# Hybrid encoder block on one core: low halves of the front-half weights subtracted on VectorE instead of GpSimd

## Chip, cores and metric

One core of a Trainium2 chip. The metric is the device time of one execution in microseconds. Engines are called PE (TensorE), DVE (VectorE), ACT (ScalarE), POOL (GpSimd) and SP (the queue that issues the DMAs).

## What is computed

One layer of a streaming encoder on 1024 tokens of width 1024, all in f32:

```
h = x @ w_in
ya = chunked attention over 8 heads, with a relative bias
yb = gated, 31-tap causal depthwise convolution, LayerNorm, swish
yc = gated DeltaNet, 4 heads, chunks, sequential state
mix = sum_b sigmoid(gate_b) * (y_b @ w_branch[b])
x = LN1(alpha * x + mix @ w_out)
x = LN2(alpha * x + relu(x @ w_up)^2 @ w_down + sigmoid(x @ w_pg) * (p @ w_pp))
```

## The kernel before, in words

**Split products.** A matmul takes its operands as fp32r. To keep f32 accuracy each operand is held as a high part, `hi`, the copy rounded to fp32r, and a low part, `lo = src - hi`; a product is three matmuls: hi by hi, hi by lo, lo by hi. The helper `split_lo(eng, lo, src, hi)` (L115, subtraction on L116) makes the low part on whichever engine is passed: `V` is VectorE, `G` is GpSimd.

**Weights of the front half.** `wload` (L118) takes a raw, a hi and a lo tile from a pool (2 raw, 6 hi and 6 lo buffers; 2 of each for the side products by `fload`, L137) and calls `wsplit` (L126): DMAs into raw on SP (L131), the hi copy on ACT (L133), the low part on GpSimd (L134). Each tile holds 512 columns by 128 partitions, 528 in `v_proj(0)`. The products `v_proj` (tiles wv), `qk_proj` (wq, wk), `dn_proj` (wc), the side products `side_glu` and `side_proj` (fa, fg) and `merge` (wbr) all come this way. Outside it are the first product, `z_start`, and everything after the merge: the output projection, the gate product and the MLP, which use other helpers, some with GpSimd.

**Order of the work.** The program is written as stages: z; attention (four pairs of heads); DeltaNet, head by head; merge of the three branches; output projection and what follows. The framework's scheduler makes each engine's list from this, with a priority by the place in the program and a model of what each operation takes. Each engine then executes its list strictly in order. The side products are given the lowest priority, so they are filled in wherever the list of PE would otherwise wait: their 1600 matmuls and transposes (PSUM tiles fj, tb, tq) lie among attention and DeltaNet and are used up before the merge is under way.

**A DeltaNet head.** `dn_proj` makes c (q, k, v after a 4-tap convolution on DVE, L431, L435). `dn_s1` transposes them (PSUM tiles tk, L480, and tv, L490) and makes the chunk matrices. `dn_inv` inverts 32x32 blocks by 31 steps on DVE, each L553 and then L554 on the tiles tm and X. `dn_s2` puts the inverse together (px, py, L578). `dn_scan` walks 8 chunks: a matmul with the state (L631), a subtraction on DVE (L632), a matmul (L635), the new state on DVE (L640), and the output (L633, L642, then ACT L643, L644). `dn_out` normalises: L648 on DVE, a power on POOL (L190), L655 on DVE, 8 transposes (PSUM tile to, L659), L660 on DVE, and stores to DRAM (yc_d, L661). Meanwhile the inverse of the next head and the product of the one after it run.

**Merge.** `merge(b)` loads a branch's output back from DRAM (`yload`: L719; hi copy on ACT, L720; low part on DVE) as four tiles of 128 rows, and multiplies them by 8 weight tiles, wbr20 to wbr27 for b = 2 (PSUM tile pbr, L164). The fourth tile of branch 2 is the output of the last DeltaNet head, so no product of merge 2 can end before it is there. Four PSUM banks hold these sums.

**The 31-tap convolution** of branch b, `b_conv`, is 240 operations on DVE (L676), also of the lowest priority; softmax rows are scaled on POOL (L307).

Of the kernel before, what the change touches and what calls it, by code (L numbers as in the profile page):

```python
# [54 lines left out]
def hybrid_block(ctx, tc, x, xT, pT, w_in, relb, conv_w, conv_b, cln_g, cln_b, dnw, a_log, dt_bias,  # L55
# [3 lines left out]
    V, S, G, PE, SY = nc.vector, nc.scalar, nc.gpsimd, nc.tensor, nc.sync  # L59
# [26 lines left out]
    def slot(shape, dt=F32, name="g"):  # L86
        return gp.tile(shape, dt, tag="g", bufs=NSLOT, name=name)
# [27 lines left out]
    def split_lo(eng, lo, src, hi):  # L115
        eng.tensor_tensor(lo, src, hi.bitcast(F32), ALU.subtract)  # L116

    def wload(src, kt, cols, name, tag="w", width=528, bufs=(2, 6)):  # L118

        n = kt * cols  # L120
        raw = wp.tile([P, width], F32, tag=tag + "r", bufs=bufs[0], name=name + "r")[:, :n]
        hi = wp.tile([P, width], F32R, tag=tag + "h", bufs=bufs[1], name=name + "h")[:, :n]
        lo = wp.tile([P, width], F32R, tag=tag + "l", bufs=bufs[1], name=name + "l")[:, :n]
        return wsplit(src, raw, hi, lo, kt)

    def wsplit(src, raw, hi, lo, kt):  # L126
        rv = raw.rearrange("p (k c) -> p k c", k=kt)
        c0 = 0
        for s in (src if isinstance(src, list) else [src]):
            w = s.shape[-1]  # L130
            SY.dma_start(rv[:, :, c0:c0 + w], s)  # L131
            c0 += w
        S.activation(hi, raw, AF.Copy)  # L133
        split_lo(G, lo, raw, hi)  # L134
        return hi.rearrange("p (k c) -> p k c", k=kt), lo.rearrange("p (k c) -> p k c", k=kt)

    def fload(src, kt, cols, name):  # L137
# [790 lines left out]
    for k in range(2):  # L928
        hi = slot([P, T], F32R, name="pth")
        lo = slot([P, T], F32R, name="ptl")  # L930
        raw = slot([P, T], name="ptr")
# [436 lines left out]
```

## Time and profile before

| | |
|---|---|
| median of 3 runs | 1928.42 us (1927.6 to 1931.17) |
| profiled execution, its own time | 1930.17 us |
| span of its trace | 1928.2 us |
| PE busy | 1848.2 us (96%) |
| DVE busy | 1254.8 us (65%) |
| ACT busy | 831.8 us (43%) |
| POOL busy | 449.9 us (23%) |

Stretches and waits are given in us from the start of the span. A busy time is that of an engine's instructions; a wait is idle time of an engine, put down to whatever released it. An engine's `x` counts are instructions; f32 matmuls of 128 columns stand twice in the trace where the program's list has them once.

### The profile page before, as it was taken

The numbers are of one execution on the slowest core, as the hardware profiler recorded it, in microseconds if no ns is written. First come the engines' busy times: TensorE is split into PE (matmuls) and PEld (weight loads), VectorE is DVE, ScalarE is ACT, GpSimd is POOL, SyncE is SP. The second block draws the span as 40 slices with busy tenths as digits, with TensorE's granted clock in tenths as the row PEclk, the third lists the DMA queues.
The fourth block names the chain that finished last, engine by engine and source line by source line (L and its number), as shares of the span: only waits on it lengthen the run. The fifth ranks groups of instructions, "written<-read, shape, count | busy, mean of one in ns | idle before, by whom it ended". The sixth has DMA issues, their size and how long they took to land. (4 is left out here: it accounts for less than half of the span.)

```text
span 1928.2 us, 25795 instructions
## 1 busy us (share of the span) xinstructions
PE 1848.2 (96%) x9265; PEld 1545.3 (80%) x9265; DVE 1254.8 (65%) x2203; ACT 831.8 (43%) x1516; POOL 449.9 (23%) x373
## 2 busy tenths in 40 slices
PE   8999999999998989989999999999999998999996
PEld 7988888778777868777888998678888887878885
DVE  3249859999957856665367548783433336876978
ACT  4454444445324333443354226445555554333333
POOL 2123433234322222222112133222232320000001
PEclk9999999999999989999999999999999999999998
DMA  6212222232342323243364535763232359347133
GB/s 202 82 49 73 74 64 68 71 89 77 87 129 61 98 72 104 66 132 92 125 199 158 168 112 180 267 224 123 96 125 94 126 196 330 139 153 256 72 114 126
DMA packets 207792, 244.67 MB, mean 127 GB/s; under 512 B 23792, under 2 KB 126256, under 8 KB 207664
## 3 DMA queue, kind: packets, MB, share of 16 engines
q1 hardware_dynamic: 207664, 243.03, 39.4%
q8 instruction: 73, 1.20, 0.3%
q14 instruction: 55, 0.45, 0.1%
HBM read 183.17 MB, written 59.80 MB: 126 GB/s over the span
## 5 line engine op out<-in xcount | busy, mean ns | idle before, releaser
L676 DVE SCALAR_TENSOR_TENSOR ca<-ci,cw_s,ca 128x512 f32<-128x512 f32 x240 | 213.3, 889 | 3.8
L986 PE MATMUL pda<-bh,ah 128*128 128x512 f32 x256 | 97.3, 396 | 8.3 <-DVE x L1258 8.3
L987 PE MATMUL pda<-bl,ah 128*128 128x512 f32 x256 | 101.2, 395 | 1.2 <-DVE bl L116 1.2
L190 POOL TENSOR_TENSOR mv<-mv,nhalf 128x1 f32<-128x1 f32 x16 | 19.7, 1235 | 351.7 <-DVE mv L683 351.7
L988 PE MATMUL pda<-bh,al 128*128 128x512 f32 x256 | 101.1, 395 | 0.0
L307 POOL TENSOR_SCALAR st<-st,mx 128x640 f32<-128x640 f32 (+2 forms) x64 | 58.8, 919 | 176.7 <-DVE mx L306 156.6
L304 ACT ACTIVATE st<-st,mx 128x640 f32<-128x640 f32 (+2 forms) x64 | 44.5, 696 | 114.2 <-DVE mx L300 114.1
L1163 DVE TENSOR_TENSOR r<-puc,r 128x512 f32<-128x512 f32 x16 | 11.1, 691 | 106.9 <-PE puc L988 106.9
L986 PE MATMUL pdb<-bh,ah 128*128 128x512 f32 x192 | 72.9, 396 | 6.3 <-ACT bh L1216 5.5
L987 PE MATMUL pdb<-bl,ah 128*128 128x512 f32 x192 | 75.5, 393 | 0.0
L988 PE MATMUL pdb<-bh,al 128*128 128x512 f32 x192 | 75.2, 392 | 0.0
L1216 ACT ACTIVATE ah<-draw 128x1024 fp32r<-128x1024 f32 x30 | 31.8, 1059 | 94.0 <-PE pdb L987 30.9
L986 PEld LDWEIGHTS pda<-bh,ah 128*128 128x128 f32 x256 | 49.1, 192 | 19.2 <-ACT x L1266 4.8
L987 PEld LDWEIGHTS pda<-bl,ah 128*128 128x128 f32 x256 | 49.1, 192 | 11.9 <-DVE bl L116 1.7
L988 PEld LDWEIGHTS pda<-bh,al 128*128 128x128 f32 x256 | 49.0, 191 | 10.4
L554 DVE TENSOR_TENSOR X<-X,tm 32x31 f32<-32x31 f32 (+15 forms) x124 | 51.9, 418 | 3.0
L771 ACT ACTIVATE sgl<-sgl 128x512 f32<-128x512 f32 x48 | 30.2, 631 | 53.4 <-DMA sgl<-sg_d 47.7
L553 DVE TENSOR_TENSOR tm<-X 32x31 f32<-32x31 f32 (+15 forms) x124 | 51.1, 412 | 3.0
L431 DVE SCALAR_TENSOR_TENSOR c<-pc,dnw_s,c 128x511 f32<-128x511 f32 (+2 forms) x72 | 52.5, 731 | 0.1
L116 DVE TENSOR_TENSOR al<-draw,ah 128x1024 fp32r<-128x1024 f32 x30 | 36.5, 1216 | 23.2 <-ACT ah L1216 23.0
L334 ACT ACTIVATE ph<-tp 128x512 fp32r<-128x512 f32 (+2 forms) x72 | 37.0, 525 | 33.4 <-PE tp L330 29.3
L986 PEld LDWEIGHTS pdb<-bh,ah 128*128 128x128 f32 x192 | 36.4, 190 | 14.6 <-ACT bh L1216 6.0
(1609 smaller groups left out, 6190.4 us busy)
## 6 DMA issues: line engine op xcount, KB each, us to landing
draw<-h_d SPq DMA_DIRECT2D x46, 512.0 KB, 5.3
wu<-in_w_up_dram SPq DMA_DIRECT2D x32, 512.0 KB, 3.9
h_d<-r SPq DMA_DIRECT2D x64, 256.0 KB, 2.1
draw<-in_w_down_dram SPq DMA_DIRECT2D x30, 512.0 KB, 4.7
sg_d<-fs SPq DMA_DIRECT2D x48, 256.0 KB, 2.1
sgl<-sg_d SPq DMA_DIRECT2D x48, 256.0 KB, 3.0
wg<-in_w_pg_dram SPq DMA_DIRECT2D x36, 256.0 KB, 4.4
cb<-in_w_down_dram SPq DMA_DIRECT2D x16, 512.0 KB, 8.0
```

The lines of the kernel that those rows point to most:

```text
L116: eng.tensor_tensor(lo, src, hi.bitcast(F32), ALU.subtract)
L304: S.activation(st[:, :nk], st[:, :nk], AF.Exp, scale=-1.0, bias=mx[:, nm:nm + 1], accum_out=mx[:, 2:3])
L307: G.tensor_scalar(st[:, :nk], st[:, :nk], mx[:, 3:4], 1.0, ALU.mult, ALU.mult)
L334: S.activation(ph[:, :n], tp[:, :n], AF.Copy)
L431: V.scalar_tensor_tensor(acc[:, 512 * hf + s_:512 * hf + 512], pp[:, :512 - s_], cw[:, 3 - s_:4 - s_], acc[:, 512 * hf + s_:512 * hf + 512 ...
L553: V.tensor_tensor(tv, bc_last(L, ncol), bc_mid(R, nr), ALU.mult)
L554: V.tensor_tensor(X3[:, jj + 1:32, 0:ncol], X3[:, jj + 1:32, 0:ncol], tv, ALU.subtract)
L676: V.scalar_tensor_tensor(acc, t[:, H - s_:H - s_ + 512], cw_s[:, i, H - s_:KB - s_], acc, ALU.mult, ALU.add)
L986: PE.matmul(out_, lhsT=ah, rhs=bh, start=first, stop=False, skip_group_check=True)
L987: PE.matmul(out_, lhsT=ah, rhs=bl, start=False, stop=False, skip_group_check=True)
L988: PE.matmul(out_, lhsT=al, rhs=bh, start=False, stop=last, skip_group_check=True)
L1216: S.activation(hi, src, AF.Copy)
```

## The change

`wsplit` passes `V` where it passed `G`. Its 136 calls' subtractions move from POOL's list to DVE's; DMAs, hi copies, tiles and buffer counts stay.

```diff
@@ def wsplit(src, raw, hi, lo, kt):
             SY.dma_start(rv[:, :, c0:c0 + w], s)
             c0 += w
         S.activation(hi, raw, AF.Copy)
-        split_lo(G, lo, raw, hi)
+        split_lo(V, lo, raw, hi)
         return hi.rearrange("p (k c) -> p k c", k=kt), lo.rearrange("p (k c) -> p k c", k=kt)
```

The scheduler orders all engines anew. Three places follow.

**DVE, in the inverse of a DeltaNet head (tiles X and tm, L553 and L554), while the projections wc of a later head are made.** Before:

```order
L553 TENSOR_TENSOR tm<-X 32x255
L554 TENSOR_TENSOR X<-X,tm 32x15x17
L553 TENSOR_TENSOR tm<-X 32x252
L554 TENSOR_TENSOR X<-X,tm 32x14x18
L553 TENSOR_TENSOR tm<-X 32x247
```

Now:

```order
L116 TENSOR_TENSOR wc210l<-wc210r,wc210h 128x512
L553 TENSOR_TENSOR tm<-X 32x255
L554 TENSOR_TENSOR X<-X,tm 32x15x17
L553 TENSOR_TENSOR tm<-X 32x252
L554 TENSOR_TENSOR X<-X,tm 32x14x18
L116 TENSOR_TENSOR wc214l<-wc214r,wc214h 128x512
L553 TENSOR_TENSOR tm<-X 32x247
```

The subtractions stand between the steps of the inverse; POOL had them in its own list.

**PE, at the transposes tv of DeltaNet head 2, beside the end of the scan of head 0 (scano, to).** Before:

```order
L694 MATMUL tb_2435<-ident_72,bcv_2433 128x128 x4
L642 MATMUL scano_7031<-c20_6221,aT0_6291 128x128
L490 MATMUL tv_7391<-ident_72,c22_7291 128x128 x4
L480 MATMUL tk_7406<-ident_72,c12_7214 128x128 x4
L659 MATMUL to_7042<-ident_72,c20_6221 128x128 x4
```

Now:

```order
L164 MATMUL fj_2498<-xh7_97,fg20h_2465 128x512
L164 MATMUL fj_2498<-xl7_98,fg20h_2465 128x512
L164 MATMUL fj_2498<-xh7_97,fg20l_2466 128x512
L490 MATMUL tv_7391<-ident_72,c22_7291 128x128 x3
L659 MATMUL to_7042<-ident_72,c20_6221 128x128 x4
L659 MATMUL to_7050<-ident_72,c20_6221 128x128 x4
L490 MATMUL tv_7391<-ident_72,c22_7291 128x128
```

Between the same L642 and the first tv there were no side products; now there are 32 of fg20, of which the last three are shown. The side products stand earlier against the heads from here on: 61 more of them are ahead of the scan of head 2.

**PE, at the end of the last head (tiles scan, scano, to), in the merge.** Before:

```order
L164 MATMUL pbr_9237<-yh_8961,wbr16l_9233 128x512
L164 MATMUL pbr_9237<-yh_8970,wbr16h_9232 128x512
L164 MATMUL pbr_9237<-yl_8971,wbr16h_9232 128x512
L659 MATMUL to_8564<-ident_72,c23_7922 128x128 x4
L659 MATMUL to_8572<-ident_72,c23_7922 128x128 x4
L164 MATMUL pbr_9237<-yh_8970,wbr16l_9233 128x512
L164 MATMUL pbr_9255<-yh_8943,wbr16h_9232 128x512
```

Now:

```order
L631 MATMUL scan_8552<-S_8547,c13_7845 128x128
L633 MATMUL scano_8553<-S_8547,c03_7768 128x128
L642 MATMUL scano_8553<-c23_7922,aT3_7992 128x128
L659 MATMUL to_8564<-ident_72,c23_7922 128x128 x4
L659 MATMUL to_8572<-ident_72,c23_7922 128x128 x4
L164 MATMUL pbr_9357<-yh_9342,wbr20h_9352 128x512
L164 MATMUL pbr_9403<-yh_9342,wbr21h_9398 128x512
L164 MATMUL pbr_9357<-yl_9343,wbr20h_9352 128x512
```

yh_9342 and yl_9343 are the fourth tile of branch 2, made of what dn_out stores after these very transposes. Before, 37 matmuls of the merge stood between the last L642 and the transposes, and 46 between the transposes and the first use of the fourth tile. Now there is none at either place: the last scan has moved back by 110 matmuls of the merge, which stand ahead of it.

## Rows read from the trace of the kernel before

**Rows 1.** Windows: us, busy (instructions) of each engine, granted clock, DMA.

```profile
core 0: us, PE busy (x) PEld busy (x) DVE busy (x) ACT busy (x) POOL busy (x), PEclk, DMA share, GB/s
...
360.00:540.00 180.00, 173.25 (x880) 143.15 (x879) 156.96 (x299) 81.76 (x182) 65.98 (x52) 0.99 0.29 82
540.00:900.00 360.00, 330.33 (x1722) 274.83 (x1722) 248.03 (x618) 132.68 (x329) 84.31 (x71) 0.96 0.32 93
900.00:1073.00 173.00, 172.13 (x832) 141.16 (x832) 98.95 (x153) 73.98 (x136) 29.84 (x22) 1.00 0.48 157
```

**Rows 2.** Waits of PE, first 1090 us: us in total, times, longest.

```profile
PE scan L631 <- DVE S L640: 7.2, 5, 3.8
...
PE tv L490 <- ACT tk L485: 3.1, 1, 3.1
...
PE tk L480 <- ACT tk L485: 2.3, 1, 2.3
...
PE fj L164 <- POOL fg04l L116: 1.5, 1, 1.5
```

**Rows 3.** Windows of L116 alone: us, DVE busy, POOL busy (columns that have any).

```profile
0.00:1073.00 1073.00, 116.70 (x177) 189.66 (x136) 0.98 0.34 100
...
540.00:900.00 360.00, 0.00 (x0) 53.55 (x42) 0.96 0.32 93
```

**Rows 4.** Line 116: shapes, with ns of one, min/median/max.

```profile
L116 DVE TENSOR_TENSOR pl<-tp,ph x72: 403/672/694, 118.4 to 535.6; 128x512 fp32r<-128x512 f32 x40, 128x384 fp32r<-128x384 f32 x16, 128x256 fp32r<-128x256 f32 x16
...
L116 DVE TENSOR_TENSOR yl<-yr,yh x24: 678/684/995, 901.0 to 1031.7; 128x512 fp32r<-128x512 f32 x24
```

**Rows 5.** Line 676, the same.

```profile
L676 DVE SCALAR_TENSOR_TENSOR ca<-ci,cw_s,ca x240: 722/752/1858, 152.5 to 529.6; 128x512 f32<-128x512 f32 x120
```

**Rows 6.** The page's costliest groups: busy, mean ns of one, idle before.

```profile
L676 DVE SCALAR_TENSOR_TENSOR ca<-ci,cw_s,ca 128x512 f32<-128x512 f32 x240 | 213.3, 889 | 3.8
```

**Rows 7.** Timeline in the inverse: start, us, engine, line.

```profile
600.81 0.31 DVE L554 TENSOR_TENSOR X<-X,tm 32x156 f32<-32x156 f32 x1
...
601.38 1.30 POOL L116 TENSOR_TENSOR fg15l<-fg15r,fg15h 128x512 fp32r<-128x512 f32 x1 [7.61 <-ACT fg15h L133]
...
601.48 1.35 DVE L554 TENSOR_TENSOR X<-X,tm 32x135 f32<-32x135 f32 x1
```

**Rows 8.** One window, columns as in rows 1.

```profile
600.00:625.00 25.00, 18.87 (x94) 15.41 (x93) 15.38 (x35) 12.83 (x43) 5.65 (x5) 0.86 0.28 74
```

**Rows 9.** Matmuls of L164 in the merge: PE busy, PEld busy, granted clock, DMA.

```profile
1040.00:1070.00 30.00, 30.00 (x131) 24.31 (x130) 1.00 0.45 144
```

**Rows 10.** Timeline from the last scan to the merge's use of it.

```profile
1009.37 0.38 PE L642 MATMUL scano<-c,aT 128*128 128x128 f32 x2
...
1011.24 0.35 ACT L643 ACTIVATE c<-scano,nv 128x128 f32<-128x128 f32 x1
...
1012.22 2.02 POOL L190 TENSOR_TENSOR r<-ss,nhalf 128x8 f32<-128x8 f32 x1 [5.13 <-DVE ss L648]
...
1014.27 2.38 DVE L655 TENSOR_TENSOR c<-c,r 128x512 f32<-128x512 f32 x2 [1.54 <-POOL r L190]
...
1018.17 1.03 PE L659 MATMUL to<-ident,c 128*128 128x128 f32 x8
...
1020.07 1.40 DVE L660 SCALAR_TENSOR_TENSOR c<-to,ng_s,z 128x512 f32<-128x512 f32 x2
...
1021.08 0.93 SPq L661 DMA_DIRECT2D yc_d<-c  x2
...
1025.63 0.32 SPq L719 DMA_DIRECT2D yr<-yc_d  x1
...
1029.71 0.69 DVE L116 TENSOR_TENSOR yl<-yr,yh 128x512 fp32r<-128x512 f32 x1 [5.60 <-ACT yh L720]
...
1030.46 0.50 PE L164 MATMUL pbr<-yl,wbr20h 128*128 128x512 f32 x1 [0.23 <-DVE yl L116]
```

**Rows 11.** Line 661, the stores of a head's output: time to landing.

```profile
DMA to landing us min/median/max: 2.0/2.0/4.6
```

## The prediction

> **What bounds the kernel now.** I read the busy times by stretch first, then PE's waits, then the timeline at those places of the list where the order has changed. The reader is to see three things.
>
> First, PE is the bound almost everywhere: in the merge, 900 to 1073 us, it is busy 172.1 of 173.0 us; in the DeltaNet stretch, 540 to 900 us, 330.3 of 360.0, and in the end of attention, 360 to 540 us, 173.3 of 180.0 [rows 1]. PE's work does not change. So the change can only alter PE's waits (6.8, 29.7 and 0.9 us in these stretches) and what the clock loses behind them.
>
> Second, hardly any wait is for a low part made by GpSimd: the largest is 1.5 us. The others are for DVE's chains in the scans, 7.2 us in 5 waits, and for ACT at the head's transposes, 3.1 and 2.3 us [rows 2]. Speeding up the subtraction itself is worth little.
>
> Third, the last head's output reaches the merge just in time: behind the last scan's matmuls at 1009.37 the output is normalised, transposed, stored, loaded back and split, and the first matmul on its low part starts at 1030.46, having waited 0.23 us [rows 10]. PE worked through that whole stretch because merge matmuls stood beside it.
>
> **The change, part by part.**
>
> *The subtraction.* 136 of them took POOL 189.66 us, 1.39 each [rows 3]; on DVE one of this shape, both inputs in SBUF, takes 0.69 us [rows 4]. DVE gets 136 x 0.69 = 94 us more. Against it stands what GpSimd had cost DVE: in the inverse, a step of 0.31 us is followed by one of 1.35 us that began 0.10 us after a POOL subtraction and ended with it [rows 7]. The convolution's operation has a median of 0.752 us, a maximum of 1.858 us [rows 5] and a mean of 0.889 us [rows 6], an excess of 240 x 0.137 = 33 us. An operation that reads a product from PSUM does not show it: 0.694 us at most [rows 4]. In the DeltaNet stretch 42 subtractions [rows 3], each costing a DVE that is busy 248 of 360 us [rows 1] 1.04 us when they meet, give 42 x 0.69 x 1.04 = 30 us. I take 65 us of relief (a few more outside), so DVE has 29 us more to do than before, not 94. The bounds are no relief, +94, and relief by every one, 94 - 136 x 1.04 = -47 us. I cost it at nothing on the path, since DVE is idle 31% of the DeltaNet stretch and 43% of the merge; the cover is thin from 360 to 540 us, where DVE is busy 157 of 180 us [rows 1]. If it goes, the price is that of the third rival.
>
> The Trainium skill, in "GPSIMD Engine Reference", section 8, Key points, says that GpSimd shares its SBUF interfaces with VectorE and contends with its instructions that have two SBUF inputs. Both lengthened operations here have two and the one that is not lengthened has one, so the trace agrees. By that rule alone, met every time, DVE would come out 47 us shorter instead of 29 longer.
>
> *POOL* loses a queue that stood ahead of its softmax scaling and powers. I take nothing for these: their waits were for DVE. The 1.5 us of PE for GpSimd goes, -1.5, or comes back as a wait for DVE, 0. SP has the same DMAs and ACT the same copies. A new wait arises on DVE, for ACT's hi copy, and what is queued behind it (scan steps, inverse steps) would wait too; the subtraction's new place in the list lies mostly ahead of its use, so I take nothing and price it as a rival.
>
> *The order: the last head.* This is the largest term. Before, 37 merge matmuls stood between the last scan and the transposes, and 46 from there to the first use of the fourth tile. Now none does; only L642, 8 transposes and two matmuls on the high part are left, so PE must wait out the chain. Seen, it lasted from 1009.37 to 1029.71 + 0.69 = 1030.40, 21.0 us [rows 10]. What was delay in the lists falls away: ACT came 1.5 us after the matmul (I leave 0.3), -1.2; the two L655 took 2.38 instead of 1.38, -1.0; PE came to the transposes 1.5 us after L655's end at 1016.65, -1.5; DVE to L660 0.9 us after the transposes' end, -0.9. Left are 16.4 us. The store took 4.55 us until the load could be issued, with a median landing of 2.0 us [rows 11]: with that it would be 13.9. I take 15.2. PE works about 1.9 us of it; the subtraction before the last L642 and the second half of the tile add some 1.1 us (an estimate from the durations of these operations). That is 14 us of waiting, 12 to 16 by the two ends.
>
> After a wait PE runs slower: from 600 to 625 us it is idle 6.1 us and the mean granted clock is 0.86, a mixture of the two levels, 1.2 and 2.4 GHz, which costs 0.14 x 25 = 3.5 us [rows 8]. I add 2 us, between 0 and 3.5. Sum of this place: **+16 us**, 12 to 19.
>
> *The order: earlier.* The 110 matmuls that now stand ahead of the last scan are worth 110 x 30/131 = 25 us of PE [rows 9]. They are not new work but come earlier, and where they fall into a wait it is recovered. Two such places I can name: 32 side products stand before the tv transposes, 7.3 us, over a wait of 3.1, and the side products fg15 now lie between the two tk groups, over 2.3 [rows 2]: -5.4. With less idle time some of the 3.5 us that the clock cost here returns [rows 8]: -3. The scan waits stay: in both lists the steps of a scan still stand directly behind each other. With the 1.5 us of GpSimd: **-10 us**. The ends are 0 (the chain on DVE moves back by as much as was filled in) and -25 (all falls into waits).
>
> *Sum:* 16 - 10 + 0 = **+6 us**. Against the profiled execution, 1930.17 us for a span of 1928.2, that is 1936.2; the median of the runs, 1928.42, lies 1.75 us below it, so I predict **1934.4 us**. About 0.2% (3.9 us) can be told from no change.
>
> **The rivals.**
>
> *The waits are filled and the lists are kept better (faster).* If the list before was made without the lengthening by GpSimd (no row shows what its model holds), DVE ran behind it; now the subtractions stand in DVE's own list. In the DeltaNet stretch 29.7 us of waits stand [rows 1]. If nearly all 25 us fall into waits, the sum is 16 - 25 = -9, 1919.5 us. It decides for faster where more than 20 us are recovered. For it: the lengthened steps lie in the inverse, on the chain of a head [rows 7]. Against it: the scan waits are of dependent steps. The rule of the Trainium skill named above speaks for this case.
>
> *The two come out even.* Recovered 16 for 16: 1928.4 us, give or take 4. It needs half of the scan waits to go too [rows 2].
>
> *DVE becomes the bound (slower still).* A subtraction at the head of DVE's list waits for its copy, and scan steps queue behind it. Say the relief is 33 us in the convolution and only 19 in the inverse: then DVE has 94 - 52 = 42 us more. The two dense stretches are half of the 1073 us, and DVE is busy there 405 of 540 us [rows 1]; 42 x 0.5 x 0.75 = 16 us would lie on the path. With the 16 of the last head and the 10 recovered that is 1928.4 + 16 - 10 + 16 = 1950 us, or 1946 if a fourth of it falls into waits that are there anyway. It decides once DVE's lists have no idle time left ahead of the scans.
>
> That the subtractions don't move is excluded by the list: all 136 are on DVE.
>
> **How the numbers follow.** The forecast has 0.45, its own range 1930.5 to 1939: slower 0.36, same 0.09. The faster rival 0.25: faster 0.24, same 0.01. Even 0.18: same 0.14, faster 0.02, slower 0.02. DVE as the bound 0.12, all slower. Sums: faster 0.26, same 0.24, slower 0.50. The range, 1919 to 1946 us, leaves out the outer halves of the first and the third rival.
>
> **What would show it.** Right: one wait of 11 to 15 us of PE in the merge, at the first matmul on the fourth tile of branch 2, put down to ACT's copy, with a lower granted clock behind it; the tv and tk waits gone; the convolution's mean near 0.77 us; steps of the inverse without 1.3 us ones; no POOL work of L116 before the merge's end. Wrong: that wait under 8 us, waits of the DeltaNet stretch under 10 us or over 35, or time changed after the merge, whose list is nearly the same.

## The result, and the profile after

The change made the kernel faster, not slower: 1898.18 us in the median of 4 runs (1894.09 to 1902.91) against 1928.01 us (4 runs, 1922.92 to 1931.17), a ratio of 0.9842 with a 95% interval of 0.9824 to 0.986. The forecast of 1934.4 us has the wrong sign, and 1898 lies below its range. The profiled execution took 1894.09 us, the lowest of the four.

The page of the kernel after, its span and its part 1 (busy time, share of the span, instructions), and the convolution's group of its part 5:

```profile
span 1892.4 us, 25829 instructions
...
PE 1832.1 (97%) x9265; PEld 1538.8 (81%) x9265; DVE 1269.4 (67%) x2339; ACT 835.4 (44%) x1518; POOL 270.8 (14%) x237
...
L676 DVE SCALAR_TENSOR_TENSOR ca<-ci,cw_s,ca 128x512 f32<-128x512 f32 x240 | 186.1, 775 | 2.8
```

DVE took over 136 subtractions and is busy only 14.6 us longer than before (1254.8). Neighbouring DVE records overlap (by 0.07 us at 877.95 in the timeline further down), and a busy time counts the overlap once. Added up one by one, DVE's instructions took 1359.9 us before and 1390.0 now: 30.1 more, of which the 136 subtractions are 95.5, so the others gave back 65.4 us. The convolution gave back 27.2 of them (213.3 before [rows 6], 186.1 now) and the two steps of the inverse 20.9. For one of these, before and then after (busy, mean ns of one, idle before):

```profile
L554 DVE TENSOR_TENSOR X<-X,tm 32x31 f32<-32x31 f32 (+15 forms) x124 | 51.9, 418 | 3.0
```

```profile
L554 DVE TENSOR_TENSOR X<-X,tm 32x31 f32<-32x31 f32 (+15 forms) x124 | 40.9, 330 | 2.6
```

The span shrank by 35.8 us, and PE's idle time makes 19.7 of them: 1928.2 - 1848.2 = 80.0 before, 1892.4 - 1832.1 = 60.3 after. The other 16.1 us are busy time for the same work. The mean granted clock rose from 0.984 to 0.987, which is 30.9 - 24.6 = 6.3 us by 1 minus the clock times the span. That is the most that the clock can explain, since a part of the low clock falls where PE is idle. The remaining 10 us I cannot split by rows; matmul ends are modelled, so stalls between matmuls need not show as idle time.

Windows of the kernel after, columns as in [rows 1]; the merge ends 30 us earlier, so its window is shorter:

```profile
360.00:540.00 180.00, 180.00 (x943) 152.16 (x942) 162.39 (x344) 85.20 (x186) 35.16 (x31) 1.00 0.31 91
540.00:900.00 360.00, 347.43 (x1818) 289.39 (x1817) 246.90 (x657) 144.23 (x350) 30.07 (x27) 0.98 0.35 101
900.00:1043.00 143.00, 132.57 (x652) 109.33 (x651) 91.76 (x151) 57.72 (x106) 1.90 (x2) 0.96 0.46 150
```

Against [rows 1], PE's idle time went from 6.75 us to nothing in the end of attention and from 29.7 to 12.6 us in the DeltaNet stretch, where the clock is 0.98 in place of 0.96. In the merge it rose from 0.9 to 10.4 us, at 0.96 in place of 1.00. The waits of PE up to the merge's end (total, times, longest):

```profile
PE pbr L164 <- ACT yh L720: 7.7, 2, 6.7
...
PE to L659 <- DVE c L655: 3.5, 1, 3.5
PE tv L490 <- ACT tk L485: 3.5, 2, 3.1
...
PE scan L631 <- DVE S L640: 1.6, 4, 0.8
```

The scan wait on L631 fell from 7.2 to 1.6 us [rows 2], and no wait is for GpSimd. The two that grew, for yh and at the transposes L659, are the end of the last head. Here is its chain in the timeline of the kernel after (start, us, engine, line; in brackets the idle time before it), and two windows, in its wait and behind it:

```profile
992.83 0.49 PE L642 MATMUL scano<-c,aT 128*128 128x128 f32 x2 [0.15 <-DVE c L632]
...
996.10 1.29 DVE L655 TENSOR_TENSOR c<-c,r 128x512 f32<-128x512 f32 x2 [1.82 <-POOL r L190]
...
996.85 1.32 PE L659 MATMUL to<-ident,c 128*128 128x128 f32 x8 [3.52 <-DVE c L655]
...
998.32 1.92 SPq L661 DMA_DIRECT2D yc_d<-c  x2
1001.37 0.93 SPq L719 DMA_DIRECT2D yr<-yc_d  x2
...
1004.20 1.36 ACT L720 ACTIVATE yh<-yr 128x512 fp32r<-128x512 f32 x2 [10.12 <-DMA yr<-yc_d]
...
1004.88 0.80 PE L164 MATMUL pbr<-yh,wbr20h 128*128 128x512 f32 x1 [6.71 <-ACT yh L720]
```

```profile
1000.00:1005.00 5.00, 0.12 (x1) 0.12 (x1) 0.14 (x1) 0.70 (x2) 0.00 (x0) 0.50 0.45 160
...
1005.00:1015.00 10.00, 10.00 (x37) 7.95 (x38) 9.11 (x14) 4.49 (x8) 0.00 (x0) 0.83 0.25 79
```

PE waits 3.52 and then 6.71 us, as the new order makes it do. The clock is at 0.50 by the end of the wait, where that costs nothing, and the 10 us of full work behind run at a mean of 0.83, which costs 1.7 us.

Where the front half ends shows in the first product of the output projection (PSUM tile pout: ns min/median/max, first and last start), first before, then after:

```profile
L164 PE MATMUL pout<-wo0h,mh x32: 278/283/283, 1072.8 to 1094.1; 128*128 128x256 f32 x32
```

```profile
L164 PE MATMUL pout<-wo0h,mh x32: 277/283/283, 1042.8 to 1064.1; 128*128 128x256 f32 x32
```

It starts 30.0 us earlier, about the difference of the medians (29.8). The profiled run, the fastest of its kernel, is another 5.8 us shorter behind that point, and I explain nothing by those.

**What I had not read.** I named 7.2 us of PE's waits for DVE. The same list of before has more of them, 29 us over all its rows, the largest being:

```profile
PE sc L296 <- DVE mx L300: 5.7, 3, 2.9
...
PE scan L635 <- DVE c L632: 4.5, 4, 2.6
PE pc L164 <- DVE halo L438: 3.6, 1, 3.6
```

In the kernel after, PE waits 9.5 us for DVE up to the merge's end, 3.5 of them at the last head. Several of these waits, which I took for waits of dependent steps, have another cause, and the trace of before shows it. At the last wait on L631, DVE, POOL and PE, in the kernel before:

```profile
875.55 0.40 DVE L554 TENSOR_TENSOR X<-X,tm 32x247 f32<-32x247 f32 x1
875.88 1.26 POOL L116 TENSOR_TENSOR fg25l<-fg25r,fg25h 128x512 fp32r<-128x512 f32 x1 [1.97 <-ACT fg25h L133]
875.99 1.42 DVE L553 TENSOR_TENSOR tm<-X 32x240 f32<-32x240 f32 x1
877.34 0.68 DVE L696 BATCH_NORM_STATS2 bst<-tb 128x6 f32<-128x512 f32 x1
877.95 0.32 DVE L640 SCALAR_TENSOR_TENSOR S<-S,egl,scan 128x128 f32<-128x128 f32 x1
878.32 0.49 PE L631 MATMUL scan<-S,c 128*128 128x128 f32 x2 [2.11 <-DVE S L640]
```

A GpSimd subtraction starts at 875.88; the inverse step of another head that starts 0.11 us later takes 1.42 us in place of 0.40; and the scan's own step L640 stands behind it in DVE's list. PE waits 2.11 us, about half of it the 1.02 us of that hold-up. The same is to be seen at 856.35 (an L553 of 1.20 us beside a subtraction, then 2.64 us of PE's waiting for L632) and in attention at 342.04 (four convolution operations in 5.33 us beside subtractions, then 2.88 us for L300). But it does not show everywhere. The longest wait on L631, 3.8 us, has no lengthened step just ahead of it: DVE waited for a DMA before the transposition that stands ahead of L640 in its list.

```profile
698.79 1.30 DVE L587 STREAM_TRANSPOSE TT<-T 128x512 f32<-128x512 f32 x2 [2.70 <-DMA T<-inv]
700.01 0.30 DVE L640 SCALAR_TENSOR_TENSOR S<-S,egl,scan 128x128 f32<-128x128 f32 x1
...
700.38 0.80 PE L631 MATMUL scan<-S,c 128*128 128x128 f32 x2 [3.80 <-DVE S L640]
```

So the timeline shows the mechanism at single places, and what it is worth in all is left to the experiments.

### The profile page after: what moved, and what is told of

Same layout as the page of the kernel before. It is cut to its first block, busy times and chain, and to the rows that moved or that the text cites. A ratio compares the mean times of both kernels' runs of the same rounds, so it can differ in the third digit from the quotient of the medians.

```text
span 1892.4 us, 25829 instructions
## 1 busy us (share of the span) xinstructions
PE 1832.1 (97%) x9265; PEld 1538.8 (81%) x9265; DVE 1269.4 (67%) x2339; ACT 835.4 (44%) x1518; POOL 270.8 (14%) x237
## 5 line engine op out<-in xcount | busy, mean ns | idle before, releaser
L676 DVE SCALAR_TENSOR_TENSOR ca<-ci,cw_s,ca 128x512 f32<-128x512 f32 x240 | 186.1, 775 | 2.8
L307 POOL TENSOR_SCALAR st<-st,mx 128x640 f32<-128x640 f32 (+2 forms) x64 | 68.2, 1066 | 392.0 <-DVE mx L306 338.4
L1216 ACT ACTIVATE ah<-draw 128x1024 fp32r<-128x1024 f32 x30 | 31.8, 1059 | 92.0 <-PE pdb L987 30.9
L988 PEld LDWEIGHTS pda<-bh,al 128*128 128x128 f32 x256 | 48.8, 190 | 10.2
L116 DVE TENSOR_TENSOR al<-draw,ah 128x1024 fp32r<-128x1024 f32 x30 | 36.6, 1221 | 21.6 <-ACT ah L1216 21.6
L986 PEld LDWEIGHTS pdb<-bh,ah 128*128 128x128 f32 x192 | 36.4, 190 | 14.6 <-ACT bh L1216 5.8
L737 ACT ACTIVATE fs<-fj 128x512 f32<-128x512 f32 x48 | 28.2, 588 | 39.8 <-PE fj L164 29.5
L116 DVE TENSOR_TENSOR pl<-tp,ph 128x512 fp32r<-128x512 f32 (+2 forms) x72 | 42.7, 595 | 3.2 <-ACT ph L334 2.7
```

The lines of the kernel that those rows point to most:

```text
L307: G.tensor_scalar(st[:, :nk], st[:, :nk], mx[:, 3:4], 1.0, ALU.mult, ALU.mult)
L676: V.scalar_tensor_tensor(acc, t[:, H - s_:H - s_ + 512], cw_s[:, i, H - s_:KB - s_], acc, ALU.mult, ALU.add)
L737: S.activation(t, r, func)
L986: PE.matmul(out_, lhsT=ah, rhs=bh, start=first, stop=False, skip_group_check=True)
L988: PE.matmul(out_, lhsT=al, rhs=bh, start=False, stop=last, skip_group_check=True)
L1216: S.activation(hi, src, AF.Copy)
```

## The experiments

**Theory 1:** a GpSimd subtraction holds up the DVE operations with two SBUF inputs that meet it; since DVE works its list in order, this delays the steps that PE waits for, and being rid of it brought the time. **Theory 2:** the new order (side products earlier, merge products ahead of the last scan) fills PE's waits, and the subtraction's engine matters only by causing that order.

**1. Hold-ups put back, order nearly kept.** A second subtraction on GpSimd, whose result nothing uses, behind the one on VectorE.

```diff
         split_lo(V, lo, raw, hi)
+        split_lo(G, raw, raw, hi)
```

> As the change, and GpSimd makes a second subtraction of each of the 136 weight tiles, written over the raw tile and used by nobody. PE's list is much like that of the change (no merge matmul between the last scan and its transposes). Theory 1, GpSimd's two-input operations hold up DVE's, and the time came from being rid of that: the convolution's mean returns from 0.775 to over 0.85 us, waits of PE return in attention (over 6 us) and DeltaNet (over 22 us), and the time is 1918 us or more. Theory 2, the new order of the lists brought the time, with the subtractions in DVE's own list: GpSimd's extra work costs under 8 us, 1898 to 1906 us.

Measured: 1938.26 us (4 runs, 1932.71 to 1939.3), ratio to the kernel before 1.0057 (1.0038 to 1.0077). That is 40 us above the kernel after, for 136 instructions whose results no product uses. Its windows (lines from 135 on stand one further), and its inverse steps X (L555 here) alone (DVE busy, clock, DMA):

```profile
360.00:540.00 180.00, 175.13 (x892) 145.52 (x893) 173.06 (x334) 85.86 (x191) 72.03 (x57) 0.99 0.29 83
540.00:900.00 360.00, 331.66 (x1726) 275.57 (x1725) 268.91 (x652) 132.30 (x325) 86.79 (x71) 0.96 0.32 94
```

```profile
0.00:1080.00 1080.00, 47.74 (x124) 0.98 0.33 97
```

PE's idle time is back to 4.9 and 28.3 us, close to the 6.75 and 29.7 of before [rows 1], the 124 steps take 47.7 us, where the kernel after has 40.92, and the convolution's mean is 0.860 us. Up to there the order is nearly that of after: ahead of the scan of head 2 stand 1447 of the 1600 side products here, 1440 after and 1379 before. At the last head it is not, and the expectation was wrong in that: 33 merge matmuls stand between the last L642 and the transposes, as 37 did before. One other thing differs: the raw tile is held until GpSimd is done, so loads can start later. PE's waits for a half of one of the 136 weight tiles, of which the kernel after has none, add up to 4.4 us, so that explains little of the 40. Experiments 2 and 8 don't have it.

**2. GpSimd's instruction without inputs, order of before.**

```diff
-        split_lo(G, lo, raw, hi)
+        G.memset(lo.bitcast(F32), 0.0)
```

> As before the change, but the low parts of the 136 front-half weight tiles are left out: GpSimd fills them with zeros instead, an operation with no input. DVE has no more to do than before and PE's list is much like that of before (merge matmuls on both sides of the last transposes). Theory 1 (GpSimd's two-input operations hold up DVE): the convolution's mean falls below 0.80 us, PE's waits in attention fall from 9.6 to under 4 us and in DeltaNet from 29.7 to under 18, with no long wait in the merge, and the time is 1885 to 1903 us. Theory 2 (the order): the list is that of before, so the waits stay, 1918 to 1930 us.

Measured: 1883.73 us (1882.77 to 1884.77), ratio 0.9778 (0.9762 to 0.9795), faster than the kernel after. Its DeltaNet window, and its timeline at a GpSimd instruction in the inverse:

```profile
540.00:900.00 360.00, 350.42 (x1899) 292.09 (x1898) 226.11 (x628) 144.94 (x351) 52.43 (x70) 1.00 0.34 101
```

```profile
550.83 0.53 POOL L134 MEMSET wc200l<- 128x512 f32 x1 [1.97 <-PE pc L164]
550.99 0.24 DVE L554 TENSOR_TENSOR X<-X,tm 32x87 f32<-32x87 f32 x1
551.26 0.27 DVE L553 TENSOR_TENSOR tm<-X 32x112 f32<-32x112 f32 x1
```

Both steps run at their usual length beside the GpSimd instruction. PE nearly keeps its old order (39 merge matmuls between the last L642 and the transposes), waits 9.6 us in place of 29.7, and the clock is 1.00. Theory 2 falls: the old order alone is not what cost the time. The low parts are also ready sooner here (0.53 us in place of 1.39), but PE had waited only 1.5 us for one [rows 2]. A third of these products multiplies zeros here, as in experiment 8; no run shows whether that alone changes the clock.

**3 and 4. Halves of the change.** The 64 side products' subtractions (fa, fg) on VectorE, the other 72 on GpSimd; then the reverse.

```diff
-        return wsplit(src, raw, hi, lo, kt)
+        return wsplit(src, raw, hi, lo, kt, V if tag == "f" else G)
```

> Only the 64 subtractions of the side products (fg, fa) move to DVE; the 72 of wv, wq, wk, wc and wbr stay on GpSimd. PE's list is like that of before. Theory 1: about half of what holds DVE up is gone, most of it in attention; PE's waits in attention fall to under 5 us, and the time is 1905 to 1918 us. Theory 2: the list is that of before, so 1922 to 1932 us.

> The reverse: the 72 subtractions of wv, wq, wk, wc and wbr move to DVE, the 64 of the side products stay on GpSimd. PE's list is like that of the change, with the wait at the last head. Theory 1: half of the hold-up stays, in attention most of it; PE's waits there are 5 us or more, and the time is 1908 to 1922 us. Theory 2: the list is that of the change, so 1895 to 1905 us.

Measured: 1905.27 us (ratio 0.9887, 0.9869 to 0.9905) and 1903.76 us (0.9887, 0.9863 to 0.9911): each half brings over two thirds of what the whole does. The third lies at the lower end of what theory 1 expected and far from theory 2's range. The fourth misses theory 1's range and lies in theory 2's, so the times alone don't decide between the two there. PE's idle time fits theory 1: from 540 to 900 us it is 23.3 us in the third, whose DeltaNet weights stay on GpSimd, and 10.6 in the fourth; from 360 to 540 us it is 1.1 in the third and 6.6 in the fourth, whose side products stay there. At the last head the third has the order of before, the fourth that of after. Their merge windows, the third's and the fourth's:

```profile
900.00:1043.00 143.00, 142.75 (x702) 117.48 (x701) 82.10 (x129) 59.95 (x111) 25.64 (x19) 1.00 0.49 160
```

```profile
900.00:1043.00 143.00, 133.31 (x646) 109.92 (x645) 88.30 (x148) 58.72 (x110) 3.29 (x2) 0.95 0.43 143
```

PE idles 9.7 us and the clock is 0.95 in the second of them, 0.2 us at 1.00 in the first. So the wait of the last head comes with the order, whichever weights GpSimd makes, and it is a cost that the change pays.

**5. The last head without its round trip.** The fourth tile of branch 2 is taken from SBUF, where `dn_out` leaves it; its store and its load fall away.

```diff
+            if h < CH - 1:
-            SY.dma_start(yc_d[h][:, sl], O[:, sl])
+                SY.dma_start(yc_d[h][:, sl], O[:, sl])
...
-            yr = slot([P, T], name="yr")
+            yr = kept if kept is not None and i == 3 else slot([P, T], name="yr")
...
-    merge(2, yc_d, False, True)
+    merge(2, yc_d, False, True, st[CH - 1]["vb"])
```

> As the change, but the output of the last DeltaNet head isn't stored and loaded back: merge 2 makes high and low part from the tile in SBUF. The wait at the first matmul on the fourth tile (6.7 us for the high part, after 3.5 us at the transposes) has the store and the load in it, 1021.08 to 1029.05 us before, 8 us. If the chain is the cause, the 6.7 us wait falls to under 1.5 us and the time to 1889 to 1894 us. Rival: with the shorter chain the scheduler's list fits no better and the wait moves into the scan or the transposes, 1896 to 1901 us.

Measured: 1893.08 us (5 runs, 1889.86 to 1893.76), ratio 0.981 (0.9791 to 0.9829). It is the first version that leaves nothing out and beats both kernels, by 35 and by 5 us; its runs all lie below those of the kernel after, though the intervals of the two ratios overlap a little (0.9824 to 0.9829). Its waits of PE at the merge (L722 is the copy that was L720):

```profile
PE to L659 <- DVE c L655: 3.5, 1, 3.5
...
PE pbr L164 <- ACT yh L722: 1.2, 2, 0.7
```

The wait of 6.7 us is gone, the one at the transposes stays.

**6 and 7. Does it hold elsewhere?** Both start from experiment 5. In one the subtractions that GpSimd still makes in the back half move to VectorE, in the other the softmax scaling.

```diff
-        hi, lo = hilo(raw, name, G)
+        hi, lo = hilo(raw, name, V)
...
-        return hilo(w, f"wg{n}{k}", G if k % 2 else V)
+        return hilo(w, f"wg{n}{k}", V)
...
-        hi, lo = hilo(src, f"wu{n}", eng, v4)
+        hi, lo = hilo(src, f"wu{n}", V, v4)
```

> The kernel without the last head's round trip (1893.08 us), with the low parts that GpSimd still makes in the back half (from 1043 us on: output projection, gate and up weights) made by VectorE too; nothing is left out. Theory 1 (a hold-up costs time only where TensorE waits for the list that is held up): from 1043 to 1580 us TensorE was busy for 527.9 of 537 us in that kernel, so at most 9 us can come back, and since its idle time there is put down to other things, I expect 1893 within 4 us. Rival (every subtraction taken from GpSimd is worth about the same: the front gave some 40 us for 136): with about 95 more the time falls by 15 us or more, to 1878 or less. Third (VectorE's own list becomes too long there): it rises above 1898.

```diff
-            G.tensor_scalar(st[:, :nk], st[:, :nk], mx[:, 3:4], 1.0, ALU.mult, ALU.mult)
+            V.tensor_scalar(st[:, :nk], st[:, :nk], mx[:, 3:4], 1.0, ALU.mult, ALU.mult)
```

> The kernel without the last head's round trip (1893.08 us), with the softmax scaling of the attention's scores (64 instructions with one tensor input, 63 us of GpSimd between 112 and 510 us) on VectorE; nothing is left out. Theory 1: from 50 to 540 us TensorE already works for 489.9 of 490 us, so there is nothing to gain, and 1893 within 3 us holds as long as VectorE carries the added 25 to 45 us; it is busy for 161.8 of 180 us from 360 to 540, so waits of some us may come there, up to 1900. Rival (any GpSimd instruction that reads from SBUF holds VectorE up, and being rid of these too brings time): 1888 or less.

Measured: 1893.25 us (1890.94 to 1894.56) and 1890.82 us (1886.41 to 1894.65), neither to be told from experiment 5. The window of the up product in the sixth, after the same window of the fifth:

```profile
1270.00:1580.00 310.00, 303.41 (x1314) 248.26 (x1313) 119.52 (x158) 161.21 (x270) 76.02 (x55) 0.99 0.42 142
```

```profile
1270.00:1580.00 310.00, 303.85 (x1317) 248.56 (x1316) 145.37 (x209) 162.43 (x273) 0.00 (x0) 0.99 0.42 140
```

GpSimd's 76 us are gone from it and PE's idle time is the same 6 us. There were hold-ups to lose: the 94 subtractions that moved take some 65 us on VectorE, and the sum of its instructions rose by 40.9 us only, from 1389.9 to 1430.8. So some 24 us of hold-ups went and brought nothing: they cost nothing where the list that is held up is not waited for. VectorE was not at its limit either.

**8. One input in place of two, order of before nearly.**

```diff
-        split_lo(G, lo, raw, hi)
+        G.tensor_scalar(lo, raw, 0.0, 1.0, ALU.mult, ALU.mult)
```

> The kernel before, with GpSimd writing each of the 136 low parts with an instruction that reads one tensor (raw times zero) in place of the subtraction, which reads two; the low parts of these weights are left out of the products by it, as in the kernel that fills them with zeros and took 1883.73 us. Theory 1, as the Trainium skill words it in the page GPSIMD Engine Reference, section 8 (contention through shared interfaces), does not say whether one input is enough. If GpSimd must read two tensors to hold VectorE up: 1884 to 1892. If any read is enough: about 1910 to 1930, with operations of the inverse of over 1 us beside such an instruction. Between the two, 1892 to 1910, if one input holds VectorE up for a part of the time: the softmax scaling, which has one input, took 1.1 us each and its removal gained no more than 2 us.

Measured: 1890.76 us (1889.16 to 1897.79), ratio 0.9792 (0.9778 to 0.9806), inside the first range. But its timeline at such an instruction does not say that one input is harmless:

```profile
639.00 0.41 DVE L553 TENSOR_TENSOR tm<-X 32x252 f32<-32x252 f32 x1
639.36 0.62 POOL L134 TENSOR_SCALAR fg16l<-fg16r 128x512 fp32r<-128x512 f32 x1 [7.54 <-issue]
639.44 0.80 DVE L554 TENSOR_TENSOR X<-X,tm 32x252 f32<-32x252 f32 x1
```

The step lasts 0.80 us in place of 0.41 and ends 0.26 us after GpSimd's instruction does, which fits a start held back to about that end. It is held up by 0.39 us, where the step at 875.99 was held up by 1.02. What has shrunk is the length of the instruction, 0.62 in place of 1.3 us. The steps L554 take 42.6 us in all here, 41.1 in experiment 2, 51.9 before. So my question was put wrongly: how long the instruction of GpSimd lasts matters, and the time can't tell its inputs from its length.

## Why the prediction was wrong

*What bounds the kernel:* right. PE's work is the same, and the time came from its waits, its clock and the 10 us that stay unsplit.

*The subtraction on DVE:* the size was right, the conclusion wrong. The relief came out at the 65 us that I took, and the sum of DVE's instructions at 30 us more for the 29. In parts, the convolution gave 27 for 33 and all else 38 for 32. The convolution's mean is 775 ns where I expected 0.77 us. But "I cost it at nothing on the path" is **the step that failed**, and with it "the scan waits stay": being rid of the hold-ups was worth some 41 us of PE's time, as worked out below. I argued from the idle share of DVE in a stretch. What counts is whether the operations held up stand ahead of one that PE waits for, and the timeline of DVE and POOL at several of PE's waits showed that they did. I had found the hold-up in the inverse [rows 7] and read the scan waits from PE's list only.

*POOL:* right. The wait of 1.5 us for a low part is gone, and DVE became no bound.

*The last head, +16:* right in mechanism, too high in sum. PE waits 10.2 us there where I took 14 (the largest single wait, 6.7 us, is below the 11 to 15 that I named, since I had not split it at the transposes). The chain from the last L642 to the first product took 1004.88 - 992.83 = 12.05 us; I took 15.2 and an added 1.1 us, of which PE would work 1.9. The clock costs the 2 us that I added, nearly: 1.7 us behind the wait. The 3.5 us by which I bounded it count the low clock of PE's idle time too, which costs nothing. Together that is 9.5 us more waiting than before, plus 1.7: +11, under my 12 to 19.

*The order earlier, -10:* this is where the missing time is. With +11 for the last head, the front's -30.0 us leave **-41** for everything else. Of the two waits that I named, tv is still there with 3.1 us and tk is gone from the list; "the scan waits stay" is wrong, 7.2 to 1.6 us on L631, with those on L635 for DVE's L632 little changed at 4.5 and 3.7. Experiment 2 has 46.2 us less up to the first pout (1026.6 for 1072.8) in nearly the order of before, without the subtractions' hold-ups and without the last head's wait, and experiment 1 has 45.1 us more than the kernel after (1087.9 for 1042.8) with the hold-ups back. So the hold-ups are enough for the 41; what the earlier side products filled by themselves I can't show to be anything.

*The rivals:* the fast one named the lists that ran behind and the rule of the Trainium skill, and its direction was the right one. I priced it by the 25 us of matmuls that could fill waits, not by the hold-ups' own length, and so stopped at 1919.5. DVE as the bound is excluded by experiments 6 and 7, which gave it still more. One of my signs of being wrong came true, the wait under 8 us, but by luck: it lies at 6.7 because the wait is split in two, and not because of the step that failed. The sign meant for that step, waits in the DeltaNet stretch under 10 us, did not come true at 12.6.

## What to carry to other kernels

Where two engines hold each other up, don't weigh the lost time against the idle share of the slower list: go to each wait of the bounding engine, and read back along the list it waits for to see whether a lengthened operation stands in it. An operation on a spare engine is not free because nobody waits for its result; a kernel with nearly the same order up to the last head was 40 us slower with 136 unused subtractions in it. And when a scheduler makes a new order, look for what it gives away: here the end of the last head, 11 us, of which keeping its tile in SBUF brought back 5.

## What was not expected of the hardware

A GpSimd instruction that only writes (the memset, 0.53 us) left steps of 0.24 and 0.27 us as they are, one that reads one tensor (0.62 us) held a step of two inputs back by 0.39 us, and the subtraction, which reads two (1.3 us), held one back by 1.02 us; both steps ended 0.26 or 0.27 us behind the GpSimd instruction. The Trainium skill says in "SBUF — State Buffer", section "Who interferes with whom", that a VectorE instruction with two SBUF inputs contends with a GpSimd instruction that reads SBUF and not with one that only writes it. The trace agrees on both. Of VectorE's two-port modes the same section of the Trainium skill says that whichever issues first has the shared ports for the whole instruction. The held steps here look the same, with two inputs. Had I gone by the length of the instruction and the place of the steps, a part of the price was there to be read: 1.02 us at 875.99, in front of a step for which TensorE waited.
